# Last FFN in a written order, two weight tiles ahead, with three column groups computed from seven products in both halves of their sum

## The chip, the cores and the metric

The kernel runs on one core of one Trainium2 chip. The metric is the time of one execution on the device in microseconds, the median of several runs.

## The reference, and what of it matters here

The program is one residual block of a streaming encoder on 256 rows (tokens) of width 2048, all in float32: an FFN, a token mixer and a second FFN, each followed by a layer norm, with shift, scale and gate rows made from a conditioning vector. The change lies in the second FFN, the last stage:

```python
y = _swiglu(modulate(x, 2), ffn2_w13[l], ffn2_w2[l])          # (silu(g) * v) @ w2
x = _layer_norm(ALPHA * x + FFN_WEIGHT * gate[:, 2, None, :] * y, ln_g[l, 2], ln_b[l, 2])
```

`_swiglu` multiplies the 256x2048 activations u by w13 (2048 x 11264: 5632 gate columns g, 5632 value columns v), takes silu(g) times v, and multiplies the result by w2 (5632 x 2048).

## The kernel before, in words

**Tiles and products.** Weights come from memory as tiles of 128 partitions x 2048 float32, 1 MB each: four slices of 128 rows by 512 columns. A float32 product is made of three fast ones. `split` (L100-112) writes a tile's high part with a cast on ScalarE (L108, names h...) and its low part with a subtraction on VectorE (L110, names l...). `mov_t` (L285-295) multiplies one weight tile with the activations of one token half (128 tokens): four slices times three matmuls (high by high, high by low, low by high), so 12 matmuls of 512 columns. I call those 12 a block product. `mov_w` does it for both token halves: 24 matmuls. There are three buffers each for high and low parts and four for raw tiles (`raw_tile`), two buffers of tag "row", six large ones of tag "slot", eight PSUM banks.

**The last FFN** is `ffn(2, ...)` (L654). Its 5632 hidden columns are 11 column groups b = 0 to 10 of 512. For each group g and v are made, silu(g) times v goes through TensorE transposes (`turn_one`, L806) into a stationary layout (a high part by ScalarE at L816, a low part by VectorE at L817), and, two at a time, turned groups meet w2 (`x_tile`, L734: one w2 tile, 24 matmuls; after every second one the two PSUM banks are added to `yacc`). Groups 0, 1 and 10 are made plainly (`rows_block`, 16 block products). Groups 2 to 9 go through `fast_block` (L704). There the first 1024 of the 2048 input rows ("quad 0": two row tiles of g and two of v, against two token halves) are computed with seven block products in place of eight, in the manner of Strassen and Winograd: sums of weight tiles are formed on VectorE (L756, L761, L766, L775, four a group) and sums of activations once, in `sums` (L683). The other 1024 rows ("quad 1") are plain: eight block products. So a group has 15 block products, four `x_tile`, eleven plus four splits.

**The order.** The instructions of `fast_block` go to the engines through plain handles (`nc.vector`, `nc.scalar`), so that the planner, which places instructions by its own costs, may set them in another order on VectorE, ScalarE and SyncE than the program writes them; TensorE's products are pinned with the handle `T`. The handles `V`, `A`, `G`, `T`, `Q` (class `Pinned`, L120) keep program order. Beside the products `tick` (L213) feeds in 16 tiles of the conditioning matrix ("ada", a multiply-and-reduce on VectorE, L210) at the rate `FFN2_RATE`. `closing` (L1026) multiplies the last three groups with w2, and `boundary` ends with the layer norm.

Of the kernel before, what the change touches and what calls it, by code (L numbers as in the profile page):

```python
# [16 lines left out]
P = 128  # L17
D = 2048
# [23 lines left out]
FFN2_RATE = 0.5  # L42
# [3 lines left out]
FAST = range(2, 10)  # L46


class Held:
# [4 lines left out]
    def __getitem__(self, key):  # L54
        return self.tile[key]
# [3 lines left out]
def block_kernel(ctx: ExitStack, tc: tile.TileContext, a: dict, out: bass.AP):  # L59
# [19 lines left out]
    wide = [False]  # L79
    n_raw = [1]  # L80
# [13 lines left out]
    def load(src, name, into=None, raw=None):  # L94

        tick()
        raw = raw or raw_tile("r" + name)
        queue().dma_start(raw, src)
        return raw, name, into
# [40 lines left out]
    def queue():  # L140

        return Q if wide[0] else nc.sync
# [511 lines left out]
    def ffn(s, w13, w2, start, following=None):  # L654
# [8 lines left out]
        b0 = RAMP // 4 if start else 0  # L663
# [5 lines left out]
        def rows_block(b, passed=None):  # L669

            i = 8 * (b - b0)
            if passed:
                pg, pv = passed[0], met(passed, w13[4:8], f"fv{s}")
            else:
                pg = [bank(f"fg{s}{b}{t}") for t in range(NT)]
                for k in range(4):
                    end = mov_w(pg, load_w(w13[i + k], f"fg{s}_{b}{k}"), uh, ul, k * 4, k == 0, k == 3)
                    if k in (1, 2):
                        turn_one(end)
                pv = [bank(f"fv{s}{b}{t}") for t in range(NT)]  # L680
                for k in range(4):
                    mov_w(pv, load_w(w13[i + 4 + k], f"fv{s}_{b}{k}"), uh, ul, k * 4, k == 0, k == 3)
# [5 lines left out]
        def sums():  # L688

            nc.gpsimd.dma_start(xd, x.tile)  # L690
            f = raw_tile("sums").rearrange("p (a b) -> p a b", b=P)
            for t in range(NT):
                tk = slice(t * P, (t + 1) * P)
                nc.vector.tensor_add(f[:, 8 * t:8 * t + 8, :], uh[:, 0:8, tk].bitcast(F32), ul[:, 0:8, tk].bitcast(F32))
            a11, a12, a21, a22 = (f[:, 4 * i:4 * i + 4, :] for i in range(4))
            nc.vector.tensor_add(a22, a21, a22)
            nc.vector.tensor_sub(a21, a11, a21)
            nc.vector.tensor_sub(a11, a22, a11)
            nc.vector.tensor_sub(a12, a12, a11)
            both = big.tile([P, 2, KT, P], F32R, tag="x", name="ws")  # L700
            nc.scalar.copy(both[:, 0], f)
            nc.vector.tensor_sub(both[:, 1], f, both[:, 0].bitcast(F32))
            return both[:, 0], both[:, 1]

        def restore():
            x.tile = tokens("x1")
            for t in range(NT):
                nc.gpsimd.dma_start(x[:, t, :], xd[:, t, :])
            scale_x()

        def fast_block(b, wh, wl):

            i = 8 * b
            gi = 4 * b // GRP - 1
            s2_, s4_, s3_, s1_ = 0, 4, 8, 12
            p1, p5 = bank(f"fa{b}"), bank(f"fb{b}")
            py = {}

            def part(ps, hl, h, k0, t, first, last):
                return mov_t(ps, hl, *h, k0, t, first, last, T, skip_group_check=not first and ps in (p1, p5))  # L720

            def fresh(k, row=False):
                return load(w13[i + k], f"fw{s}_{b}{k}", None, row_tile(f"fw{b}{k}") if row else None)

            def halves(tile, w=""):
                return split((tile[0], tile[1] + w, None), nc.scalar, nc.vector)

            def kept(ps, tag, w):
                to = sm.tile([P, 512], F32, tag=tag, bufs=2, name=f"{w}{s}{b}")
                nc.scalar.copy(to, ps)  # L730
                return to

            def x_tile(m):
                n, k = b % 2 * 2 + m // 2, m % 2  # L734
                if not k:
                    py[n] = [bank(f"py{gi}_{n}_{t}") for t in range(NT)]
                kg = 2 * gi + k
                end = mov_w(py[n], load_w(w2[kg * 4 + n], f"w2{s}_{kg}_{n}"), *hts[gi], k * 4, not k, k == 1, T)
                if k:
                    c = slice(n * 512, (n + 1) * 512)  # L740
                    for t in range(NT):
                        if gi == 0:
                            evac.append(nc.scalar.copy(yacc[t][:, c], py[n][t]))
                        else:
                            nc.vector.tensor_add(yacc[t][:, c], yacc[t][:, c], py[n][t])
                return end

            u, w = (uh, ul), (wh, wl)
            ta = fresh(0, True)
            end = part(p1, halves(ta), u, 0, 0, True, True)  # L750
            turn_one(end)
            f1 = kept(p1, "u", "fs")
            tc_ = fresh(4, b >= 4)
            end = x_tile(0)
            turn_one(end)
            nc.vector.tensor_sub(ta[0], tc_[0], ta[0])  # L756
            part(p5, halves(ta, "p"), w, s1_, 0, True, True)
            f5 = kept(p5, "gy", "ft")
            td = fresh(5)
            x_tile(1)  # L760
            nc.vector.tensor_sub(ta[0], td[0], ta[0])  # L761
            part(p1, halves(ta, "q"), w, s2_, 0, False, True)
            f2 = kept(p1, "gy", "fv")
            part(p5, halves(td), w, s4_, 0, False, False)
            x_tile(2)
            nc.vector.tensor_sub(tc_[0], td[0], tc_[0])  # L766
            part(p1, halves(tc_, "q"), w, s3_, 0, False, True)
            f3 = kept(p1, "u", "fu")
            p2, p4 = bank(f"fc{b}"), bank(f"fd{b}")
            tb = fresh(1)  # L770
            part(p2, halves(tb), u, 4, 0, True, False)
            g2_ = load_w(w13[i + 2], f"fw{s}_{b}2")
            part(p2, g2_, u, 8, 0, False, False)
            part(p4, g2_, u, 8, 1, True, False)
            nc.vector.tensor_sub(tb[0], tb[0], ta[0])  # L775
            part(p4, halves(tb, "p"), u, 4, 1, False, False)
            g3_ = load_w(w13[i + 3], f"fw{s}_{b}3")
            part(p2, g3_, u, 12, 0, False, True)
            part(p4, g3_, u, 12, 1, False, True)
            nc.vector.tensor_add(f1, f1, p2)  # L780
            nc.scalar.activation(f1, f1, AF.Silu)
            nc.vector.tensor_add(f3, f3, p4)
            nc.scalar.activation(f3, f3, AF.Silu)
            x_tile(3)
# [4 lines left out]
            if 4 * b // GRP not in hts:  # L789
                new_h(4 * b // GRP)  # L790
# [768 lines left out]
```

## Time and profile before

| what | us |
|---|---|
| median of 3 runs | 1881.79 (1880.12 to 1884.59) |
| the profiled execution | 1882.46 |
| its span, first to last instruction | 1880.7 |
| start of group 2 in it (first `fa` matmul) | 1242.96 |
| start of group 10 in it (first `fg` matmul of the group) | 1759.44 |

The profile shows one execution. Times in its rows count from the first instruction. A row of a timeline has the start, the duration, the engine, the line and the tiles, and in brackets how long the engine had been idle and what it had waited for. Busy times of TensorE overlap, so the distance from one matmul's start to the next is its price, not its duration. The chain of work that ended last names at each moment what the end depended on.

### The profile page before, as it was taken

The numbers are of one execution on the slowest core, as the hardware profiler recorded it, in microseconds if no ns is written. First come the engines' busy times: TensorE is split into PE (matmuls) and PEld (weight loads), VectorE is DVE, ScalarE is ACT, GpSimd is POOL, SyncE is SP. The second block draws the span as 40 slices with busy tenths as digits, with TensorE's granted clock in tenths as the row PEclk, the third lists the DMA queues.
The fourth block names the chain that finished last, engine by engine and source line by source line (L and its number), as shares of the span: only waits on it lengthen the run. The fifth ranks groups of instructions, "written<-read, shape, count | busy, mean of one in ns | idle before, by whom it ended". The sixth has DMA issues, their size and how long they took to land.

```text
span 1880.7 us, 21240 instructions
## 1 busy us (share of the span) xinstructions
PE 1861.4 (99%) x8495; PEld 1526.0 (81%) x8495; DVE 1561.3 (83%) x1467; ACT 895.1 (48%) x847; POOL 43.2 (2%) x68
## 2 busy tenths in 40 slices
PE   8999999999999999999999999999999999999998
PEld 5788888888888888788888887878778888888886
DVE  6899998887887987889997877789887788778776
ACT  4543444533334335756644356454544455545441
POOL 0000000000000000100000121000000000000000
PEclk9999999999999999999999999999999999999999
DMA  9989889999899987478687574768855654564662
GB/s 377 417 354 366 319 311 347 357 348 355 344 357 355 339 331 269 148 276 296 244 317 296 203 264 182 268 246 300 307 210 190 224 212 168 202 224 186 239 224 90
DMA packets 74931, 520.06 MB, mean 277 GB/s; under 512 B 8736, under 2 KB 8912, under 8 KB 13520
## 3 DMA queue, kind: packets, MB, share of 16 engines
q1 hardware_dynamic: 72144, 507.54, 71.6%
q0 software_dynamic: 960, 7.37, 1.0%
q10 hardware_dynamic: 1728, 3.80, 0.6%
q8 instruction: 66, 1.08, 0.2%
q14 instruction: 33, 0.27, 0.0%
HBM read 514.46 MB, written 4.22 MB: 276 GB/s over the span
## 4 chain that ended last, share of the span: by engine, by line
PE 92%; DVE 4%; DMA 2%; issue 1%; ACT 1%; POOL 0%; POOLq 0%; DVEq 0%; SPq 0%; ACTq 0%
PE py L133 9%; PE pj L281 5%; PE fa L133 5%; PE fb L133 4%; PE fc L133 3%; PE fd L133 3%; PE py L293 3%; PE py L294 3%; PE py L292 3%; PE pj L283 3%; PE fg L293 3%; PE fg L294 3%; PE fg L292 3%; PE fv L293 3%; PE fv L292 3%; PE fv L294 3%
## 5 line engine op out<-in xcount | busy, mean ns | idle before, releaser
L210 DVE CUSTOM_DVE_ANT_0 ada<-ada,scb,badac 128x2048 f32<-128x2048 f32 x110 | 258.0, 2345 | 39.5 <-DMA ada<-in_w_ada 39.0
L108 ACT CAST hw<-rw 128x2048 fp32r<-128x2048 f32 x81 | 155.1, 1914 | 218.0 <-DMA rw<-in_w 60.6
L110 DVE TENSOR_TENSOR lw<-rw,hw 128x2048 fp32r<-128x2048 f32 x81 | 185.1, 2287 | 55.8 <-ACT hw L108 55.0
L110 DVE TENSOR_TENSOR lfw<-rfw,hfw 128x2048 fp32r<-128x2048 f32 x48 | 109.9, 2289 | 17.2 <-ACT hfw L108 17.2
L281 PE MATMUL pj<-u,hs 128*128 128x512 f32 x512 | 122.5, 391 | 0.0
L108 ACT CAST hra<-rra 128x2048 fp32r<-128x2048 f32 x38 | 72.6, 1914 | 102.2 <-DMA rra<-in_w_r 43.1
L108 ACT CAST hfw<-rfw 128x2048 fp32r<-128x2048 f32 x48 | 91.9, 1915 | 47.8 <-PE py L133 28.2
L281 PEld LDWEIGHTS pj<-u,hs 128*128 128x128 f32 x512 | 94.3, 188 | 18.4
L133 PE MATMUL py<-lw,hth 128*128 128x512 f32 x256 | 99.8, 390 | 2.1 <-DVE lw L110 2.1
L133 PE MATMUL py<-hw,hth 128*128 128x512 f32 x256 | 100.4, 392 | 0.0
L293 PE MATMUL py<-lw,hth 128*128 128x512 f32 x256 | 99.8, 390 | 0.1
L294 PE MATMUL py<-hw,htl 128*128 128x512 f32 x256 | 99.7, 390 | 0.0
L133 PE MATMUL py<-hw,htl 128*128 128x512 f32 x256 | 99.7, 389 | 0.0
L292 PE MATMUL py<-hw,hth 128*128 128x512 f32 x256 | 97.3, 392 | 0.0
L108 ACT CAST hfg<-rfg 128x2048 fp32r<-128x2048 f32 x28 | 53.6, 1914 | 86.1 <-DMA rfg<-in_w 48.8
L108 ACT CAST hs<-rs 128x2048 fp32r<-128x2048 f32 x32 | 61.0, 1908 | 68.7 <-PE pj L281 53.6
L293 PE MATMUL fg<-lfg,u 128*128 128x512 f32 x224 | 87.4, 390 | 0.1
L294 PE MATMUL fg<-hfg,u 128*128 128x512 f32 x224 | 87.3, 390 | 0.0
L293 PE MATMUL fv<-lfv,u 128*128 128x512 f32 x224 | 87.2, 389 | 0.0
L294 PE MATMUL fv<-hfv,u 128*128 128x512 f32 x224 | 87.1, 389 | 0.0
L108 ACT CAST hfv<-rfv 128x2048 fp32r<-128x2048 f32 x28 | 53.6, 1913 | 66.7 <-DMA rfv<-in_w 41.3
L292 PE MATMUL fg<-hfg,u 128*128 128x512 f32 x224 | 84.5, 392 | 0.0
(727 smaller groups left out, 4764.4 us busy)
## 6 DMA issues: line engine op xcount, KB each, us to landing
ada<-in_w_ada SPq DMA_DIRECT2D x138, 1024.0 KB, 6.5
rw<-in_w SPq DMA_DIRECT2D x81, 1024.0 KB, 5.5
rfw<-in_w SPq DMA_DIRECT2D x50, 1024.0 KB, 4.8
rra<-in_w_r SPq DMA_DIRECT2D x45, 1024.0 KB, 7.4
rs<-in_w_s SPq DMA_DIRECT2D x32, 1024.0 KB, 5.0
rfg<-in_w SPq DMA_DIRECT2D x28, 1024.0 KB, 6.7
rfv<-in_w SPq DMA_DIRECT2D x28, 1024.0 KB, 5.5
rwo<-in_w_out SPq DMA_DIRECT2D x16, 1024.0 KB, 4.8
```

The source lines that it names most:

```text
L108: act.copy(cut(hi, w), like(raw[:, w], hi))
L110: low.tensor_sub(cut(lo, w), like(raw[:, w], lo), cut(hi, w).bitcast(F32))
L133: self.last = getattr(self.engine, op)(*args, **kw)
L210: vec.tensor_tensor_reduce(raw[:, c], raw[:, c], scb[:, c], 1.0, base, ALU.mult, ALU.add, to)
L281: nc.tensor.matmul(ps, hi[:, k * P:(k + 1) * P], both(k), start=k == 0, stop=False)
L283: nc.tensor.matmul(ps[:, 0:S], lo[:, k * P:(k + 1) * P], uh[:, k, :], start=False, stop=k == KT - 1)
L292: pe.matmul(o, acth[:, k0 + j, tk], cut(hi, w), start=first and j == 0, stop=False, **kw)
L293: pe.matmul(o, acth[:, k0 + j, tk], cut(lo, w), start=False, stop=False, **kw)
L294: end = pe.matmul(o, actl[:, k0 + j, tk], cut(hi, w), start=False, stop=last and j == 3, **kw)
```

## The change

`ffn` keeps only the first FFN. The last FFN becomes `last_ffn`, which writes out every step and gives every instruction but those of the gate rows to the pinned handles. A step is a triple: what TensorE does, what prepares its weight tile (load, sums, split), and what follows it. `flow` emits the steps; before a step goes to TensorE, the tiles of that step and of the next two that have one are prepared (`AHEAD = 3`). `beside` hangs other work (the ada tiles, the sums of activations, the gated sum) behind the preparation of certain tiles.

Groups 2, 3, 5, 7 and 9, and now 10 as well, have seven products in quad 0 (`S4`, `S2`). Groups 4, 6 and 8 (`DOUBLE`, plan `D6`) have seven in both quads, 14 block products, and take six of the pair's eight w2 tiles (X); the plan `S2` after them takes the other two. Quad 1 needs its own sums of activations (`sums(1, in_slot)`), kept in one slot and one row buffer. In the groups of `BY_DMA` two of the four sums of weight tiles a quad are made by a GpSimd DMA that adds a tile in memory onto one in SBUF (c + d for P7, a + b for P4); in the others VectorE makes all four. x goes to memory scaled and comes back by an adding DMA onto the gated `yacc`.

```diff
-FAST = range(2, 10)
+DOUBLE = (4, 6, 8)
+BY_DMA = DOUBLE
+AHEAD = 3
+S4 = "P1 t X t P5 X P6 P3 X P7 P2 G P4 G X V V"
+S2 = "P1 t G t P5 X P6 P3 G P7 P2 X P4 V V"
+D6 = "P1 t X t P5 X P6 P3 X P7 P1 P2 X P5 P4 X P6 P3 P2 X P7 P4"
...
+        def step(pe, prep=None, after=None):
+            steps.append((pe, prep, after))
+            n_prep[0] += prep is not None
+        def beside(fs, at=0, every=1):
+            for k, f in enumerate(fs):
+                extras.setdefault(n_prep[0] + at + k * every, []).append(f)
...
+        def flow():
+            hls, late, n, m = {}, [], 0, 0
+            for i, (pe, prep, after) in enumerate(steps):
+                for f in late:
+                    f()
+                while n < len(steps) and (n <= i or len(hls) < AHEAD):
+                    if steps[n][1]:
+                        hls[n] = steps[n][1]()
+                        for f in extras.get(m, ()):
+                            f()
+                        m += 1
+                    n += 1
+                pe(hls.pop(i, None))
+                late = after() or [] if after else []
...
+        def halves(tile, w="", into=None):
+            return split((tile[0], tile[1] + w, into), A, V)
...
+        def turn():
+            def pe(_):
+                b, t, sg = to_turn.pop(0)
...
+                    T.transpose(now[0][2][:, j * P:(j + 1) * P], sg[:, j * P:(j + 1) * P], ident)
+            def after():
+                b, t, ps = now.pop()
...
+                A.copy(hth[:, :, tk], ps)
+                V.tensor_sub(htl[:, :, tk], ps, hth[:, :, tk].bitcast(F32))
...
+            for n in ns:
+                yield lambda n=n: x_step(kgs[0], n, pss, 0, False)
+                yield lambda n=n: x_step(kgs[1], n, pss, 1, True, lambda: evac(n))
...
+            def keep(key, tag, q, bk="1"):
+                if q == 0:
+                    f[key] = sm.tile([P, 512], F32, tag=tag, bufs=2, name=f"f{key}{s}{b}")
+                    A.copy(f[key], ps[bk])
+                else:
+                    V.tensor_add(f[key], f[key], ps[bk])
...
+                elif w == "P7":
+                    keep("3", "u", q)
+                    if q:
+                        V.tensor_add(f["5"], f["5"], f["3"])
+                elif w == "P5" and q == quads - 1:
+                    keep("5", "gy", 0, "5")
+                elif w == "P3" and q:
+                    V.tensor_add(f["2"], f["2"], f["5"])
+                    V.tensor_add(f["2"], f["2"], ps["3"])
+                elif w == "V" and q:
+                    V.tensor_add(f["2"], f["2"], ps["5"])
+                    V.tensor_add(f["5"], f["5"], ps["1"])
...
+                        V.tensor_add(f[g], f[g], ps[key])
+                        A.activation(f[g], f[g], AF.Silu)
...
+                        def product(t=t, g=g, v=v):
+                            V.tensor_mul(f[g], f[g], f[v])
+                            to_turn.append((b, t, f[g]))
...
+            def prep(w, q):
+                if w == "P1":
+                    W["a", q] = raw(q, 0, q == 0)
+                    return halves(W["a", q])
+                if w == "P5":
+                    W["c", q] = raw(q, 4, row_c)
+                    a, c = W["a", q], W["c", q]
+                    V.tensor_sub(a[0], c[0], a[0])
+                    hl = halves(a, "p")
+                    if dma:
+                        G.dma_start(c[0], w13[i + 2 * q + 5], accum_op=ALU.add)
+                    return hl
+                if w == "P6":
+                    W["d", q] = raw(q, 5, q == 1)
+                    a, d = W["a", q], W["d", q]
+                    V.scalar_tensor_tensor(a[0], a[0], -1.0, d[0], op0=ALU.mult, op1=ALU.subtract)
+                    hl = halves(a, "q")
+                    if dma:
+                        G.dma_start(a[0], w13[i + 2 * q + 1], accum_op=ALU.add)
+                    return hl
+                if w == "P3":
+                    return halves(W["d", q])
+                if w == "P7":
+                    c, d = W["c", q], W["d", q]
+                    if not dma:
+                        V.tensor_add(c[0], c[0], d[0])
+                    return halves(c, "q")
+                if w == "P2":
+                    W["b", q] = raw(q, 1)
+                    return halves(W["b", q])
+                if w == "P4":
+                    a = W["a", q]
+                    if not dma:
+                        V.tensor_add(a[0], a[0], W["b", q][0])
+                    return halves(a, "r")
...
+        def gated_sum(t):
+            def go():
+                for n in range(4):
+                    c = slice(n * 512, (n + 1) * 512)
+                    V.tensor_mul(yacc[t][:, c], yacc[t][:, c], gate[:, c])
+                G.dma_start(yacc[t], xd[:, t, :], accum_op=ALU.add)
...
+        beside([scaled(0), scaled(1), ada, ada, ada, *sums(0, in_x), ada, ada])
+        first_group(nxt.pop())
+        plain_group(1)
+        beside([ada] * 9, 3, 3)
+        for b in range(2, n_b - 1, 2):
+            kgs = (b - 2, b - 1)
+            if b in DOUBLE:
+                xs = x_steps(kgs, range(4))
+                fast_group(b, 2, xs, D6, False)
+                fast_group(b + 1, 1, xs, S2, False)
+            else:
+                xs = x_steps(kgs, range(4))
+                for i in range(2):
+                    fast_group(b + i, 1, xs, S4, b > 2 and not DOUBLE)
+            if b == 2 and DOUBLE:
+                beside(sums(1, in_slot), -4)
+        beside([lambda: gate_rows(s, 0.5)], -4)
+        beside([gated_sum(0), gated_sum(1)], 4, 2)
...
+        es = end_steps()
+        fast_group(n_b - 1, 1, es, S2, False)
```

In a plan P1 to P7 are the seven products of a quad, in the order of their use, G and V the plain row tiles of quad 1 (both token halves, 24 matmuls), X a w2 tile, t the transposes of one token half of the group before. P5 and P6 always need a sum on VectorE ahead of their split; P7 and P4 need one where the DMA doesn't make it.

More of the change, by code (lines that the diff above doesn't have):

```diff
@@ L140, in queue @@
     def queue():
-        return Q if wide[0] else nc.sync
+        return Q if wide[0] or fixed[0] else nc.sync
     @contextmanager
@@ L662, in ffn @@
         evac = []
-        b0 = RAMP // 4 if start else 0
+        b0 = RAMP // 4
         sts = new_stats(s)
@@ L705, in restore @@
[L705 to L784, printed above, removed]
-            vs = [load_w(w13[i + 4 + k], f"fw{s}_{b}{4 + k}") for k in (2, 3)]
-            for t, ps in enumerate((p5, p1)):
-                for k in range(2):
-                    part(ps, vs[k], u, 8 + 4 * k, t, False, k == 1)
-            if 4 * b // GRP not in hts:
-                new_h(4 * b // GRP)
-            for t, h, v, ps in ((0, f1, f2, p5), (1, f3, f5, p1)):
-                nc.vector.tensor_add(v, v, ps)
-                nc.vector.tensor_mul(h, h, v)
-                to_turn.append((b, t, h))
@@ L973, in g1 @@
             grp = groups[gi]
-            if start and gi == 2:
+            if gi == 2:
                 new_h(gi)
@@ L982, in g1 @@
                 return
-            if start and gi == 3:
+            if gi == 3:
                 for t in range(NT):
```

330 lines of the change are left out of this document (243 added, 87 removed).

## The prediction

> **What bounds the kernel now.** I read the page's head first, then the busy times by stage, the chain that ended last inside the last FFN, and the timelines of VectorE and ScalarE there.
>
> ```profile
> span 1880.7 us, 21240 instructions
> PE 1861.4 (99%) x8495; PEld 1526.0 (81%) x8495; DVE 1561.3 (83%) x1467; ACT 895.1 (48%) x847; POOL 43.2 (2%) x68
> ```
>
> The stages, cut at the starts of groups 2, 5, 6 and 10 (columns: PE, weight load, DVE, ACT, POOL busy, clock, DMA share, GB/s):
>
> ```profile
> 1242.90:1441.80 198.90, 194.00 (x854) 158.49 (x853) 170.62 (x108) 102.47 (x77) 0.00 (x0) 0.99 0.68 254
> 1441.80:1505.30 63.50, 63.50 (x286) 52.60 (x285) 50.49 (x32) 32.76 (x23) 0.00 (x0) 1.00 0.54 199
> 1441.80:1759.20 317.40, 317.40 (x1422) 262.82 (x1421) 250.56 (x158) 167.34 (x118) 2.21 (x4) 1.00 0.56 206
> ```
>
> From group 5 to the end of group 9 TensorE never stops (317.40 of 317.40), and VectorE, the next one, is busy 79% (250.56). In groups 2 to 4 TensorE loses some time. The chain gives the prices of the steps:
>
> ```profile
> 1242.96 2.72 PE fa L133 x12
> ...
> 1436.38 8.16 PE fa L133 x36
> 1444.54 0.44 PE th L814 x4
> 1444.98 5.47 PE py L133 x24
> 1450.45 0.44 PE th L814 x4
> 1450.88 2.75 PE fb L133 x12
> 1453.63 5.44 PE py L133 x24
> ...
> 1508.47 5.47 PE py L133 x24
> ```
>
> A block product of 12 matmuls is 2.72 us, a step of 24 is 5.44, four transposes 0.44. A group is 15 x 2.72 + 4 x 5.44 + 0.88 = 63.4; the two `py` rows stand 63.49 apart. The `fa` row of 36 holds 24 matmuls of group 4, so group 5 begins at 1441.82, and groups 2 to 4 took 198.86 where 3 x 63.49 = 190.5 would do: 8.4 are lost there.
>
> **Removed.** Three groups and group 10 lose a block product each: 4 x 2.72 = 10.9 us of TensorE, all on the path, since TensorE is the path. If the new order also ends the loss in groups 2 to 4, 8.4 more go. So 19.3 is the most that can be won.
>
> **What the order costs.** VectorE and ScalarE now take their instructions as written. In the planner's order a sum of weight tiles stands far ahead of its split:
>
> ```profile
> 1446.74 2.29 DVE L110 TENSOR_TENSOR lw<-rw,hw 128x2048 fp32r<-128x2048 f32 x1
> 1448.94 2.29 DVE L761 TENSOR_TENSOR fw<-rfw,fw 128x2048 f32<-128x2048 f32 x1
> 1451.14 1.28 DVE L817 TENSOR_TENSOR htl<-th,hth 128x512 fp32r<-128x512 f32 x2
> 1453.35 2.29 DVE L110 TENSOR_TENSOR lfw_50q<-fw,hfw_50q 128x2048 fp32r<-128x2048 f32 x1 [0.93 <-ACT hfw_50q L108]
> 1456.39 0.69 DVE L745 TENSOR_TENSOR yacc<-yacc,py 128x512 f32<-128x512 f32 x1 [0.75 <-PE py L133]
> 1456.99 2.29 DVE L110 TENSOR_TENSOR lfw<-rfw,hfw 128x2048 fp32r<-128x2048 f32 x1
> ```
>
> ```profile
> 1450.92 0.59 ACT L816 CAST hth<-th 128x512 fp32r<-128x512 f32 x1 [3.42 <-PE th L814]
> 1451.40 1.92 ACT L108 CAST hfw_50q<-fw 128x2048 fp32r<-128x2048 f32 x1
> ```
>
> Back to back, a 128x2048 step of VectorE is 2.20 (1446.74 to 1448.94), a 128x512 step 0.60 (1456.39 to 1456.99); a cast is 1.92 and its low part starts 0.03 later. Behind the sum at 1448.94 the planner put two `htl`. In the new text sum, cast and low part are written one after the other, so VectorE stands idle for the cast, about 1.97 us, at every sum that it makes.
>
> By count alone, a pair (D6 + S2): TensorE has 14 x 2.72 + 6 x 5.44 + 0.88 = 71.6 and 7 x 2.72 + 6 x 5.44 + 0.88 = 52.6, together 124.2, where the pair before has 127.0. VectorE has 33 low parts and 8 sums (41 x 2.20 = 90.2), 28 small steps (16.8) and 8 idle casts (15.8): 122.8, or 99%. It can keep up only if it never waits for anything else.
>
> It does wait, and I followed its queue step by step. At the start of D6 (time 0: the last V of the group before ends on TensorE) the queue reads: two adds and two products (4 x 0.60 = 2.4), P5's sum 2.20, cast 1.97, low part 2.20, X2's low part 2.20, the first `htl` 0.60, P6's sum 2.20, cast 1.97, low part 2.20, the second `htl` 0.60: 18.5, and some 0.2 to see the end of V and to hand on: 18.7. The second `htl` stands behind the whole preparation of P6, because `flow` prepares P6 before it emits the second t. On TensorE P1, t, X1, t, P5 and half of X2 take 2.72 + 0.44 + 5.44 + 0.44 + 2.72 + 2.72 = 14.5, and the second half of X2 reads that `htl`. TensorE waits 4.2 us, in every even group; before, both `htl` came at 1451.14, ahead of the `py` step at 1453.63 that needs them. Queued behind it on VectorE stand P3's low part, X2's adds and all that follows.
>
> Further on in the pair, the same way: P6' of D6 needs its d in the row buffer, which P4 gives back when its low part is done (49.2 after the start). Its load, sum, cast and low part then follow with nothing between:
>
> ```profile
> L781 ACT ACTIVATE fs<-fs 128x512 f32<-128x512 f32 x8 | 5.0, 630 | 17.7 <-DVE fs L780 17.7
> ```
>
> ```profile
> rfw<-in_w SPq DMA_DIRECT2D x50, 1024.0 KB, 4.8
> xd<-x POOLq DMA_DIRECT2D x1, 2048.0 KB, 11.1
> x<-xd POOLq DMA_DIRECT2D x2, 1024.0 KB, 7.4
> ```
>
> 49.2 + 4.8 + 2.2 + 1.97 + 2.3 = 60.5, while TensorE is ready at 57.9: 2.6. In S2 the last V steps: P4's sum starts behind X8's low part (117.1), 2.2 + 1.97 + 2.2 to 123.5, then the add and the silu that close the first sum (1.2), and only then the cast and low part for V (4.2): 128.9, TensorE ready at 126.2: 2.7. The others, each from where VectorE then stands: P5' of D6, low part of X4 done at 39.9, an add, then sum, cast and low part (0.6 + 6.4): 46.9, TensorE ready at 46.0: 0.9. P5 of S2: the adds that close D6 hold VectorE until 85.3, and 6.4 more make 91.7 against 89.2: 2.5. P6: X's low part, `htl`, then again 6.4: 100.9 against 99.8: 1.1. P7: two low parts and 6.4 behind 101.8: 112.6 against 112.0: 0.6. With three small ones D6 comes to 79.7 and S2 to 60.1: 139.8, or 15.6 of waits a pair, 46.8 for three.
>
> Hidden is the traffic: D6 loads 14 tiles and adds 4 by transfers, 18 x 1.05 MB in 79.7 us, 237 GB/s, less than groups 2 to 4 had (254, at a DMA share of 0.68). SyncE's loads stay two or more preparations ahead of their casts but for that one d; if they didn't, each would cost up to the 4.8 of a load. ScalarE has 33 casts a pair and is under two thirds busy. P6's sum is a scalar-tensor-tensor now, which the trace has in no such size: I price it like the subtraction, at most like the ada step below (0.15 more).
>
> Groups 2 and 3 (S4) keep 15 products and gain nine ada tiles at fixed places and the second set of activation sums:
>
> ```profile
> L210 DVE CUSTOM_DVE_ANT_0 ada<-ada,scb,badac 128x2048 f32<-128x2048 f32 x11 | 25.8, 2348 | 8.8 <-DMA ada<-in_w_ada 8.8
> ```
>
> VectorE there has 2 x (19 x 2.20 + 8 x 0.60 + 4 x 1.97) = 109, the ada 9 x 2.3 = 20.7 and 8.8 for the sums: 138, against 127 on TensorE, so 11 at least. By the queue the waits are 10.7 in group 2 (5.3 at X2, with an ada tile in that chain too) and 10.5 in group 3 (P6 3.5, P7 2.9, P4 2.3, V 1.8): 21.2. Group 10 in S2 has the 7.6 of that plan and about half of the gated sums' eight multiplies (4.8): 10. Groups 0 and 1 take 5.44 on TensorE a step and at most 2.20 + 2.35 on VectorE: nothing.
>
> **The clock.** Before, TensorE waited once for 2.58 us, and what came behind ran slowly:
>
> ```profile
> 1240.00:1280.00 40.00, 37.42 (x163) 30.42 (x162) 35.42 (x23) 20.46 (x17) 0.00 (x0) 0.96 0.61 219
> ```
>
> ```profile
> 1263.02 0.50 PE L133 MATMUL fa<-lfw_20q,ws 128*128 128x512 f32 x1 [2.58 <-DVE lfw_20q L110]
> ...
> 1264.17 1.05 PE L133 MATMUL fa<-hfw_20q,ws 128*128 128x512 f32 x2
> 1265.02 0.63 PE L133 MATMUL fa<-lfw_20q,ws 128*128 128x512 f32 x1
> ```
>
> Matmuls 0.43 apart instead of 0.227 in a stretch whose granted clock is 0.96: 0.04 x 40 = 1.6 us for that wait. Four X2 waits of 4 us or more could cost 6.4; behind a VectorE that is late anyway I take half, 3. The Trainium skill ("TensorE: Matmul & The Clock Gate", section "Part 1: The HAM clock gate") has the clock halve after an idle window of about 3.4 us; the row shows it after 2.58. By the page's window as a least idle time the X2 waits, which two matmuls divide, would cost nothing, and the sum would be 3 lower.
>
> **The sum.** The profiled execution took 1882.46 (span 1880.7 and 1.8 around it). -10.9 - 8.4 + 21.2 + 46.8 + 10 + 3 = +61.7: 1944; it stands 0.7 above the median of the runs, so 1943.5 on that scale, and I say 1944.
>
> **The rivals.**
> *Faster.* The queue's waits are filled after all: only the counts bind. Then -19.3 + 11 = -8, 1874. For it: 122.8 is below 124.2, and ScalarE is half idle. Against: the chain at the start of D6 alone costs 3 x 4.2. It decides if all waits in groups 4 to 10 stay under 8 us together.
> *Only the openings wait.* The counts, and the X2 chain in groups 4, 6 and 8: -8 + 12.6 = +5, and 3 for the clock: 1890. For it: the waits further on hang on estimates of where VectorE stands; against: they follow from the same queue.
> *The transfers are late.* The row tile a' is summed by GpSimd's DMA from P6's low part (60.6) on, and P4's cast wants it at 72.5: 11.9 us. No adding transfer is in the trace. It moves 1 MB and reads its target besides; the nearest rows are 7.4 for 1 MB and 11.1 for 2 MB, so I take 9 to 11, and nothing is late. At 20 us, each of three D6 waits 8 more: +25, 1969. The Trainium skill ("DMA: Bandwidth & Descriptors", "Anatomy of one DMA") gives 2.0 us and bytes / 436e3 for such a transfer, as an estimate 4.4 for 1 MB, which would strike this rival; the row for 1 MB is 7.4.
>
> **How the numbers follow.** The forecast has 0.72, the late transfers 0.10, the openings alone 0.10, the faster case 0.08. The range goes from halfway between the count case and the forecast, 1909, to the late transfers with a clock cost at more waits, 1974. A measurement of this kernel tells about 0.2% (3.8 us) from no change. Faster has its 0.08; within 0.2% lies a little of the openings case (a few us less than 1890), 0.04; the rest is slower, 0.88.
>
> **What would show it.** Right: TensorE busy well under 100% from group 2 to 9; a pair near 140 us between the first P1 products of groups 4 and 6; VectorE idle about 1.9 us before each low part that follows a sum, released by ScalarE; in X2 of groups 4, 6 and 8 a wait of some 4 us that ends on `htl`; a d load that waits for the row buffer. Wrong: pairs of 124 to 127 us; `htl` done before X2's second half; VectorE under 85% busy with TensorE full; or ScalarE waiting for GpSimd's transfers at P7 or P4, which would put the loss on them.

## The result, and the profile after

| kernel | median us | runs | range |
|---|---|---|---|
| before | 1881.82 | 4 | 1880.12 to 1884.59 |
| after | 1972.41 | 4 | 1971.89 to 1973.68 |

The change makes the kernel slower: ratio 1.0481, 95% interval 1.0463 to 1.0499, 90.6 us more. The profiled execution of after took 1972.67, its span is 1970.9. Group 2 starts at 1244.01 in it (1.05 later than before), group 10 at 1827.46 (68.0 later), and the end comes 90.2 later. So groups 2 to 9 cost 67.0 us more, and what follows from group 10 on 22.2 more.

The head of after's page:

```profile
span 1970.9 us, 21259 instructions
PE 1894.8 (96%) x8447; PEld 1533.9 (78%) x8447; DVE 1606.7 (82%) x1498; ACT 916.4 (46%) x864; POOL 54.2 (3%) x80
```

TensorE has 48 matmuls fewer, the four block products that the change removes, and yet is busy 33 us longer, above all since matmuls run slowly behind waits. The share of the chain that ended last, by engine, tells who sets the pace now (TensorE held 92% of it before):

```profile
PE 70%; DVE 15%; issue 6%; ACT 6%; DMA 2%; POOL 0%; DVEq 0%; ACTq 0%; POOLq 0%; SPq 0%
```

The busy times by stage, cut at the starts of groups 2, 4, 6, 8 and 10 (columns: length, PE, weight load, DVE, ACT, POOL, clock, DMA share, GB/s):

```profile
1242.90:1393.86 150.96, 138.64 (x574) 110.52 (x573) 120.10 (x78) 69.88 (x55) 0.00 (x0) 0.94 0.57 219
1393.86:1539.58 145.72, 134.06 (x557) 106.12 (x556) 110.99 (x71) 70.28 (x49) 3.49 (x4) 0.95 0.62 206
1539.58:1683.10 143.52, 132.82 (x557) 105.67 (x556) 109.31 (x69) 70.29 (x49) 3.42 (x4) 0.96 0.62 205
1683.10:1827.46 144.36, 132.86 (x559) 105.61 (x557) 109.38 (x69) 70.34 (x50) 4.57 (x6) 0.96 0.63 211
1827.46:1970.90 143.44, 120.19 (x493) 93.93 (x491) 102.52 (x101) 45.37 (x36) 5.12 (x6) 0.94 0.46 154
```

A pair (two groups) took 127.0 before and takes 145.7, 143.5 and 144.4. In none of these stages is any engine full: TensorE stands still for some 11 us a pair, VectorE for 35, and ScalarE for half the time. That looks like a stage bound by the order in which the engines wait for each other; the experiments test it.

VectorE at the start of D6 (group 4), where the prediction followed its queue step by step (columns: start, duration, engine, line, operation, tiles; in brackets the idle time and what ended it):

```profile
1397.36 2.28 DVE L142 TENSOR_TENSOR fw<-rfw,fw 128x2048 f32<-128x2048 f32 x1
1401.70 2.29 DVE L142 TENSOR_TENSOR lfw_40p<-fw,hfw_40p 128x2048 fp32r<-128x2048 f32 x1 [2.06 <-ACT hfw_40p L142]
1403.99 2.29 DVE L142 TENSOR_TENSOR lw<-rw,hw 128x2048 fp32r<-128x2048 f32 x1
1406.19 0.68 DVE L142 TENSOR_TENSOR ht<-th,ht 128x512 fp32r<-128x512 f32 x1
1406.80 2.28 DVE L142 SCALAR_TENSOR_TENSOR fw<-fw,rfw 128x2048 f32<-128x2048 f32 x1
1411.12 2.29 DVE L142 TENSOR_TENSOR lfw_40q<-fw,hfw_40q 128x2048 fp32r<-128x2048 f32 x1 [2.04 <-ACT hfw_40q L142]
1413.33 0.68 DVE L142 TENSOR_TENSOR ht<-th,ht 128x512 fp32r<-128x512 f32 x1
```

P5's sum, 2.06 idle for its cast, two low parts, the first `ht`; then P6's sum, 2.04 idle, its low part, and only at 1413.33 the second `ht`. On TensorE the second X waits for it:

```profile
1411.63 0.50 PE L142 MATMUL py<-hw,ht 128*128 128x512 f32 x1 [2.05 <-ACT ht L142]
1411.96 0.44 PE L142 MATMUL py<-lw,ht 128*128 128x512 f32 x1
1414.07 1.22 PE L142 MATMUL py<-hw,ht 128*128 128x512 f32 x2 [1.67 <-DVE ht L142]
1415.09 0.63 PE L142 MATMUL py<-lw,ht 128*128 128x512 f32 x1
1415.51 1.05 PE L142 MATMUL py<-hw,ht 128*128 128x512 f32 x2
...
1418.50 0.63 PE L142 MATMUL f<-hfw_40q,ws 128*128 128x512 f32 x1
1418.93 0.44 PE L142 MATMUL f<-lfw_40q,ws 128*128 128x512 f32 x1
1419.21 0.63 PE L142 MATMUL f<-hfw_40q,ws 128*128 128x512 f32 x2
```

2.05 + 1.67 = 3.72 us of waiting, and behind it matmuls 0.43 apart instead of 0.227 until 1418.9. From 1262 us on the recorded clock has 16 such slow stretches ahead of the kernel's last 3 us, 13 of 3.41 us and three of 6.83, 65 us together.

The adding transfers of after (median from issue to landing in the last column):

```profile
rfw<-in_w POOLq DMA_DIRECT2D x9, 1024.0 KB, 8.1
fw<-in_w POOLq DMA_DIRECT2D x3, 1024.0 KB, 8.8
yacc<-xd POOLq DMA_DIRECT2D x2, 1024.0 KB, 10.1
```

### The profile page after: what moved, and what is told of

The parts are those of the page before. It is cut to its first block, busy times and chain, and to the rows that moved or that the text cites. A ratio compares the mean times of both kernels' runs of the same rounds, so it can differ in the third digit from the quotient of the medians.

```text
span 1970.9 us, 21259 instructions
## 1 busy us (share of the span) xinstructions
PE 1894.8 (96%) x8447; PEld 1533.9 (78%) x8447; DVE 1606.7 (82%) x1498; ACT 916.4 (46%) x864; POOL 54.2 (3%) x80
## 4 chain that ended last, share of the span: by engine, by line
PE 70%; DVE 15%; issue 6%; ACT 6%; DMA 2%; POOL 0%; DVEq 0%; ACTq 0%; POOLq 0%; SPq 0%
PE f L142 9%; PE pj L290 5%; PE py L142 4%; PE py L302 3%; PE py L301 3%; PE py L303 3%; PE pj L292 3%; DVE fw L142 2%; PE fg L302 2%; PE fg L303 2%; PE fg L301 2%; PE fv L301 2%; PE fv L302 2%; PE fv L303 2%; PE rv L765 2%
## 5 line engine op out<-in xcount | busy, mean ns | idle before, releaser
L142 PE MATMUL py<-hw,ht 128*128 128x512 f32 x656 | 217.9, 404 | 18.4 <-ACT ht L142 10.2
L142 PEld LDWEIGHTS py<-hw,ht 128*128 128x128 f32 x656 | 127.2, 195 | 49.6 <-ACT ht L142 12.1
L142 PE MATMUL py<-lw,ht 128*128 128x512 f32 x328 | 131.9, 402 | 0.9 <-DVE lw L142 0.9
L142 DVE CUSTOM_DVE_ANT_0 ada<-ada,scb,badac 128x2048 f32<-128x2048 f32 (+1 forms) x50 | 110.8, 2216 | 4.3 <-DMA ada<-in_w_ada 4.1
L302 PE MATMUL py<-lw,hth 128*128 128x512 f32 x256 | 99.8, 390 | 0.1
L303 PE MATMUL py<-hw,htl 128*128 128x512 f32 x256 | 99.7, 390 | 0.0
L301 PE MATMUL py<-hw,hth 128*128 128x512 f32 x256 | 97.3, 392 | 0.0
L119 DVE TENSOR_TENSOR ls<-rs,hs 128x2048 fp32r<-128x2048 f32 x32 | 73.0, 2282 | 11.7 <-ACT hs L117 11.6
L142 DVE TENSOR_TENSOR lra<-rra,hra 128x2048 fp32r<-128x2048 f32 x29 | 66.3, 2286 | 9.7 <-ACT hra L142 7.6
L292 PE MATMUL pj<-u,ls 128*128 128x256 f32 x512 | 66.4, 283 | 0.0
L117 ACT CAST hfg<-rfg 128x2048 fp32r<-128x2048 f32 x20 | 38.3, 1915 | 60.1 <-DMA rfg<-in_w 55.5
```

Source lines behind the costliest of these rows:

```text
L117: act.copy(cut(hi, w), like(raw[:, w], hi))
L119: low.tensor_sub(cut(lo, w), like(raw[:, w], lo), cut(hi, w).bitcast(F32))
L142: self.last = getattr(self.engine, op)(*args, **kw)
L292: nc.tensor.matmul(ps[:, 0:S], lo[:, k * P:(k + 1) * P], uh[:, k, :], start=False, stop=k == KT - 1)
L301: pe.matmul(o, acth[:, k0 + j, tk], cut(hi, w), start=first and j == 0, stop=False, **kw)
L302: pe.matmul(o, acth[:, k0 + j, tk], cut(lo, w), start=False, stop=False, **kw)
```

## The experiments

The theory was that the written order costs the time: VectorE and ScalarE take what is written, stand idle for each other behind every sum, and the transposed values stand behind the preparation of P6. The rivals: the second quad itself (more sums and splits), late adding transfers, or the clock. Each run has its own median of before beside it, 1881.8 to 1884.7; ratios are to that.

| run | median us | ratio, 95% interval |
|---|---|---|
| no group doubled | 1945.28 | 1.0335 (1.0320 to 1.0351) |
| sums on VectorE | 2004.67 | 1.0648 (1.0632 to 1.0664) |
| transposes first | 1957.32 | 1.0395 (1.0380 to 1.0411) |
| sums ahead | 1943.44 | 1.0324 (1.0307 to 1.0342) |
| waits filled | 1968.42 | 1.0465 (1.0449 to 1.0480) |
| reordered | 1929.03 | 1.0256 (1.0239 to 1.0273) |
| reordered, none doubled | 1900.81 | 1.0101 (1.0086 to 1.0117) |
| reordered, sums on VectorE | 1959.17 | 1.0410 (1.0394 to 1.0426) |
| reordered, none doubled, gated tile early | 1895.26 | 1.0064 (1.0047 to 1.0081) |
| reordered, without quad 1's sums | 1925.07 | 1.0219 (1.0204 to 1.0234) |
| end stage alone | 1959.61 | 1.0402 (1.0387 to 1.0418) |
| reordered, transposes later | 1953.86 | 1.0371 (1.0348 to 1.0393) |

### No group doubled

```diff
-DOUBLE = (4, 6, 8)
+DOUBLE = ()
```

> The written order without the second quad: DOUBLE and BY_DMA empty, all of groups 2 to 9 in S4 (15 block products). Theory of the queue (VectorE stands idle for the cast behind each sum, and the second htl stands behind P6's preparation): three block products come back, 8.2 us of TensorE, but a pair of S4 groups has 114 us of VectorE queue against 127 of TensorE, so odd groups wait about 2 us and even ones 5 to 6 with the X2 chain and a slow clock behind it: a pair takes 135 to 137 against the 144.5 measured, 24 less for three pairs, and the sums of the second quad go (3): about 1945, still 60 slower than before. Rival of the doubling (the second quad and its sums are the cost): pairs are back at 127, 1915 to 1920. Rival of the transfers (the adding transfers come late): the same 1915 to 1920.

1945.28, as the theory said. 63 us of the loss stay without a single second quad and without adding transfers of weight tiles: they belong to the written order, with what it fixes (the places of the ada tiles, the new end). The second quad adds the other 27. Both are parts of the loss.

### All sums on VectorE

```diff
-BY_DMA = DOUBLE
+BY_DMA = ()
```

> BY_DMA empty: VectorE makes the sums for P7 and P4 in groups 4, 6 and 8 too, four more a group, no adding transfer for weights. Theory of the queue: each is 2.20 us and an idle cast of 1.97 in a queue that already sets the pace, 16.7 a pair less what VectorE idles while it waits for TensorE: 8 to 14 more a pair, about 2005 in all (1995 to 2015). Rival of the transfers: they were late, so the time falls or stays: 1972 or less.

2004.67: without the transfers it is 32 us slower. They take work off VectorE. Nor are they late: from group 2 to the end of group 9 no wait of ScalarE in after's trace ends on one.

### Both transposes ahead of the first X

```diff
-S4 = "P1 t X t P5 X ..."
+S4 = "P1 t t X P5 X ..."
-D6 = "P1 t X t P5 X ..."
+D6 = "P1 t t X P5 X ..."
```

> In S4 and D6 both transposes t stand ahead of the first X (P1 t t X P5 ...), so the second htl is emitted ahead of P6's preparation; nothing else changes. Theory of the queue: the wait inside X2 in groups 2, 4, 6 and 8 (3.3 to 4.1 us in the profile) and the slow clock behind it (about 1.7) go, and later waits stay: 4 x 5 less, about 1952 (1947 to 1958). Rival of the count (VectorE's queue is full over the pair, so a wait that is taken away comes back at the next low part): under 5 us less, 1967 or more.

1957.32, 15 us less: 4.3 in groups 2 and 3, 12.8 in the three pairs (141.1, 140.2, 139.6), that is 3.4 to 4.8 each; from group 10 on 1.6 were given back. It is at the upper end of what was expected. The X2 chain costs about what the trace shows for it (waits of 3.3 to 3.7 us a pair and slow matmuls behind them), and it is a sixth of the loss.

### Each sum emitted one preparation earlier

The sum for P5, P6, P7 and P4 (with its load) goes out behind the preparation of the step before, so that VectorE has a low part between the sum and its cast.

```diff
+                        follow = next((x for x in steps[n + 1:] if x[1]), None)
+                        if follow and follow[3]:
+                            follow[3]()
```

> Each sum on VectorE (P5, P6, and P7, P4 where no transfer makes them) is emitted, with its load, right behind the preparation of the step before, ahead of that step's evacuations, and only the split at its old place: the same instructions, another order. The cast then needs no sum in front of it. Theory of the queue: the eight idle casts a pair (15.8 us) go, and the chain at the start of D6 falls from 18.7 to about 12.4 us, under the 14.5 that TensorE takes: pairs fall from 144.5 to 127 to 131, groups 2 and 3 from 150 to 130 to 135, group 10 by 6 to 8: 1895 to 1920. Rival of the doubling or of the transfers: the order of sum and split matters little, 1955 or more. Rival of the count: VectorE's busy time alone is 107 a pair, so it predicts the same as the queue here.

1943.44: missed, 29 us less instead of 50 or more. The waits at X2 of groups 4, 6 and 8 are gone, and so is P6's in group 3. But the second P6 of D6 still waits 2.2 us and the V of groups 5, 7 and 9 still 2.1, and other waits came, first of all at the transposes, which wait for the product that closes a group, now behind the sums on VectorE (TensorE's waits there from 1242 on: us in all, times, longest):

```profile
PE th L142 <- DVE f L142: 6.7, 5, 2.3
```

### The waits filled with matmuls

Small matmuls on a spare bank (24 between the halves of the second X of each pair's first group, 14 ahead of P5 and of the first V of groups 5, 7 and 9) keep TensorE busy where it waits.

```diff
+                    idle(bank(f"id{kg}"), 24)
...
+                idle(bank(f"id{w}{b}"), 14)
```

> The changed kernel with TensorE kept busy where the profile shows it waiting long: 24 small 128x128 matmuls (0.12 us each in the opening rows of the kernel before, 2.8 us together) between the two halves of X2 in groups 2, 4, 6 and 8, and 14 (1.6 us) ahead of P5 and ahead of the first V in groups 5, 7 and 9; their result is used by nothing. Theory that the halved clock is on the path: the ten or so half-clock stretches behind these waits (3.4 us, or 6.8, at half speed: 1.7 or 3.4 us lost each) go, 12 to 20 us less: 1952 to 1961. Rival, that VectorE's queue sets the time and hides a slow TensorE: 0 to 4 less, 1968 or more; if the small matmuls outlast the waits, it gets slower than 1973.

1968.42: the mean clock rises from 0.982 to 0.992, of the 65 us at half clock 31 are left, and the time falls by 4. The forecast of 12 to 20 missed. But the run doesn't settle what the half clock costs, because the fills lasted longer than meant: each small matmul leaves two records, and a fill took 5.3 us in place of 2.8, or 3.05 in place of 1.6. The X2 of group 4, VectorE's low part for it (done at 1411.69) and the fill, which TensorE is still busy with until 1412.38:

```profile
1411.01 0.68 DVE L142 TENSOR_TENSOR ht<-th,ht 128x512 fp32r<-128x512 f32 x1
```

```profile
1407.10 5.52 PE L142 MATMUL id<-ident 128*128 128x128 f32 x48
1412.38 0.48 PE L142 MATMUL py<-hw,ht 128*128 128x512 f32 x1
```

At the ten fills TensorE goes on 0.35 to 1.1 us after its tile was ready, 5.7 us together. So 17 us of lost speed came back, the fills themselves took up at least some 6 of them, and 4 were won. How many of the others a late VectorE would have cost anyway is open: the half clock costs 4 us or more, and shorter fills weren't tried.

### Reordered, with and without the second quad, and with all sums on VectorE

The sums ahead as above; what closes a group behind the next preparation; X last in S4 and S2; in the last stage the products that need group 10 last.

```diff
+S4 = "P1 t X t P5 X P6 P3 X P7 P2 G P4 G V V X"
+S2 = "P1 t G t P5 X P6 P3 G P7 P2 V P4 V X"
+D6 = "P1 t X t P5 X P6 P3 X P7 P1 P4 P2 X P5 X P6 P3 P2 X P7 P4"
...
+            for n, k in ((0, 0), (0, 1), (1, 0), (1, 1), (2, 0), (2, 1), (0, 2), (1, 2), (2, 2)):
```

> e4_sums_ahead with the remaining waits of its trace taken away by order alone: the add and silu that close a gate half, and the products, are emitted behind the next preparation and not ahead of it; the last X of S4 and S2 stands at the end, so that TensorE has work while the products are made; P4 of quad 0 stands right behind P1 of quad 1 in D6, so that the row buffer for d comes free sooner; the w2 tile that needs group 10's transposes comes later in the end. Theory of the queue: pairs fall from 137 to 126 to 131, groups 2 and 3 from 142.6 to 134 to 140, the end from 143 to 130 to 138: 1885 to 1912. Rival of the count: VectorE is busy 109 of a pair with or without this, and two tiles of lookahead are too few for D6: pairs stay above 133, 1925 or more.

> e6_reordered without the second quad (DOUBLE and BY_DMA empty, all in S4). Theory of the queue: a pair of S4 groups then takes 127 to 130, of which 127 is TensorE's own work: within 10 us of e6_reordered, which saves 8.2 of TensorE and pays for it with a fuller VectorE. Rival of the doubling: 20 or more faster than e6_reordered.

> e6_reordered with all sums on VectorE (BY_DMA empty; in D6 P2 of quad 0 stands ahead of P1 of quad 1, since the sum for P4 then needs b). Theory of the queue: four more sums a D6 are 8.8 us of VectorE a pair, without idle casts now; VectorE's sum for a pair goes from 107 to 116 of 124: 2 to 8 more a pair than e6_reordered, 6 to 24 in all. Rival of the transfers (they delay P7 and P4): not slower than e6_reordered.

1929.03, 1900.81 and 1959.17 (the last with P2 ahead of the second P1 in D6). The first missed what the theory wanted: pairs of 134 to 138 us. The second shows why. Without doubling the same order runs TensorE full. The stage of groups 4 and 5 in the reordered kernel without doubling, and that of groups 6 and 7 in the one with it:

```profile
1383.72:1511.42 127.70, 127.56 (x569) 104.79 (x568) 98.70 (x61) 65.95 (x47) 0.00 (x0) 1.00 0.51 198
```

```profile
1523.33:1658.74 135.41, 127.29 (x557) 102.06 (x556) 108.90 (x70) 70.20 (x49) 3.43 (x4) 1.00 0.65 218
```

So doubling costs 28 us in this order, 27 in the change's; it saves three products (8.2 us), so some 36 us of waits and slow matmuls come with it, 12 a pair. And the transfers are again worth 30 us.

### The gated tile earlier; the end stage alone

From group 10 on, the last product needs a w2 tile that is multiplied by the gate, and it was prepared after everything else. In the reordered kernel without doubling it now follows the first of the last three X; in the changed kernel it is prepared behind the last X tile, and the products that need group 10 come last.

```diff
-            for n, k in (..., (0, 2), (1, 2), (2, 0), (2, 1), (2, 2)):
+            for n, k in (..., (2, 0), (2, 1), (0, 2), (1, 2), (2, 2)):
...
+        beside([lambda: gated(0)], -1)
         flow()
         fine[0] = True
-        gated(0)
```

> The reordered kernel without doubling (1900.8), with the gated w2 tile that the last product needs first taken out of its place behind everything and prepared after the first of the last three X steps. There TensorE waited 6.0 us for it (5.63 for the cast, 0.40 for the low part). Theory of the queue: the end stage is long because of where work stands on VectorE, so these 6.0 us go, less up to 2 that come up as other waits: 1894 to 1898. Rival: the gated tile is late because all of VectorE's work at the end is, and the moved work delays the adds into x by as much: 1899 or more.

> The changed kernel (1972.4) with two edits in its last stage alone: the gated w2 tile that the last product needs first is prepared behind the last X step's own tile instead of after everything, and the X steps that need group 10's transposed values come after those of the other two groups. Group 10 to the end took 143.4 us against 121.3 before; of it 4.9 stand at X(0,2) behind the second transposes and 4.5 at the gated tile. Theory: both are the order of the queues, 5 to 10 less, 1962 to 1967. Rival: VectorE is late there by its amount of work, 0 to 3 less, 1969 to 1972.

1895.26 and 1959.61: 5.5 and 12.8 us less. Both are the order of the queues. The second gain is larger than expected: from group 10 on the waits below are gone, and with them most of the half clock there (13.7 us of it ahead of the last 3 us, 3.4 after the edit). In the changed kernel TensorE had waited at these places from group 10 on (us in all, times, longest), and after the edit none of these rows is left:

```profile
PE tl L301 <- ACT hw22l L142: 3.6, 1, 3.6
PE py L142 <- ACT ht L142: 2.8, 1, 2.8
...
PE py L142 <- DVE ht L142: 1.2, 1, 1.2
PE tl L302 <- DVE lw22l L142: 0.9, 1, 0.9
PE py L142 <- DVE lw L142: 0.9, 1, 0.9
```

### Without quad 1's sums

```diff
-                    V.tensor_sub(a[0], c[0], a[0])
+                    if not q:
+                        V.tensor_sub(a[0], c[0], a[0])
```

and the same for P6's sum, in the reordered kernel. The kernel leaves these two sums out, so it computes other values.

> The reordered kernel with doubling (1929.0), with the two sums that VectorE makes for quad 1 (c - a and -a - d) left out, so the values that it multiplies there are not the reference's; all loads, splits, transfers and products stay. A pair is 136.4 us with doubling and 127.8 without. Theory: doubling costs because it fills VectorE's queue; two sums of 2.2 and the casts that two of them wait for (up to 4) go from each pair: three pairs x 4.4 to 8.4 = 13 to 25 less, 1904 to 1916. Rival: doubling costs by something else that it brings (the adding transfers, the held row buffers, the longer chains of PSUM sums): at most 3 us a pair less on TensorE's path, 1920 or more.

1925.07: 4 us less where 13 to 25 were expected. The theory that doubling costs mainly by the amount of VectorE's work falls. The stage of groups 6 and 7 in this run:

```profile
1523.35:1656.00 132.65, 127.22 (x557) 103.45 (x556) 104.31 (x68) 70.39 (x49) 3.42 (x4) 0.99 0.66 222
```

VectorE has 4.6 us less to do than in the reordered kernel, and the pair is 2.8 shorter; the last one is 1.7 shorter, and the first isn't shorter at all (138.1 against 138.2).

### The transposes later

In the same reordered kernel the longest waits of a pair stand at the transposes: 3.0 in S2 behind D6, where both sums close at its very end, 1.7 to 2.1 in D6.

```diff
+S2 = "P1 t G P5 t X P6 P3 G P7 P2 V P4 V X"
+D6 = "P1 X t t P5 X P6 P3 X P7 P1 P4 P2 X P5 X P6 P3 P2 X P7 P4"
```

> The reordered kernel with doubling (1929.0), with only the places of the transposes changed: in S2 the second stands behind P5 instead of ahead of it, in D6 both stand behind the first X and P5 ahead of the second X. Leaving out quad 1's sums took only 2.7 us from a pair of 135.4, so most of the 8.6 that a pair has above one without doubling lies elsewhere: in its trace TensorE waits 2.7 and 1.7 at the transposes that follow a closed double sum (release by VectorE's product) and 0.8 at the X behind them, and one half-clock stretch follows. Theory: the doubling's price is this late closing of both sums at the end of D6, so later transposes save 4 to 7 a pair: 1907 to 1918. Rival: the closing is late because VectorE as a whole is, and the wait comes up again at the next step that it feeds: 1923 or more.

1953.86, 25 us more, and neither reading was tested cleanly: the waits at the transposes of the pairs are gone, but a new one is longer. ScalarE in group 6 of this run:

```profile
1535.63 1.91 ACT L142 CAST hfw_60p<-fw 128x2048 fp32r<-128x2048 f32 x1 [4.63 <-DVE fw L142]
1540.50 0.59 ACT L142 COPY f<-f 128x512 f32<-128x512 f32 x1 [2.96 <-PE th L142]
1540.98 1.91 ACT L142 CAST hw<-rw 128x2048 fp32r<-128x2048 f32 x1
1547.51 1.90 ACT L142 CAST hfw_60q<-fw 128x2048 fp32r<-128x2048 f32 x1 [4.61 <-DVE fw L142]
1549.31 1.07 ACT L142 CAST ht<-th 128x512 fp32r<-128x512 f32 x2
```

The copy of P1's sum waits for a buffer that the transposes give back (2.96), VectorE's next sum comes late by that, and the casts of both transposed halves stand behind the cast that waits for this sum (4.61). TensorE's X waits 6.29 for them, in each pair. The wait did come up again at the next step, as the rival had it, but on ScalarE's queue.

## Why the prediction was right, and where it was short

**Sign and mechanism: right.** 1972.4 lies in the range, near its upper end. The queue at the start of D6 came as written: idle 2.06 and 2.04 us for the casts (forecast 1.97), the second `ht` behind P6's low part, X2's wait 3.72 (forecast 4.2), worth 3.4 to 4.8 us a pair, slow matmuls included, when the order is changed. Most of the other waits named are there too, and mostly a little shorter: P6' of D6 waits 2.10 (forecast 2.6), its sum first 1.5 for a d load that had to wait for the row buffer; P5' 0.85 (0.9), P5 of S2 2.06 (2.5), V 2.10 (2.7). Those of S2's P6 and P7 (forecast 1.1 and 0.6) are missing, but for 0.8 at P6 in group 9. P6's scalar-tensor-tensor took 2.28, like the subtraction. P6' of D6 on VectorE, with the wait for d, the sum, the idle cast and the low part:

```profile
1451.57 2.29 DVE L142 SCALAR_TENSOR_TENSOR rfw<-rfw,fw 128x2048 f32<-128x2048 f32 x1 [1.51 <-DMA fw<-in_w]
1455.88 2.29 DVE L142 TENSOR_TENSOR lfw_42q<-rfw,hfw_42q 128x2048 fp32r<-128x2048 f32 x1 [2.03 <-ACT hfw_42q L142]
```

**The pairs: too low by 4.7 each.** Forecast 139.8, measured 144.5 on average: 14 us in three pairs. Of the 4.7, 2.7 are in D6 (82.4 on average, forecast 79.7) and 2.0 in S2 (62.1, forecast 60.1). It isn't the named waits: between the starts of groups 4 and 6 TensorE stands idle for 11.7 in all, where 15.6 stood. That pair exceeds the count of 124.2 by 21.5; 6.8 of the rest are 13.65 us at half clock, and 3.0 weren't followed. So the forecast put the waits too high and the slow matmuls far too low, and the two errors partly cancel. What a pair would take at full clock no run shows cleanly: with the waits filled, most of the half clock in the pairs went and they took 2.3 us less together, but the fills outlasted the waits.

**The clock: priced too low.** The sum had 3 us, from the X2 waits of four groups. The trace has 16 slow stretches, 65 us, which is 32 us of lost speed. From group 2 on TensorE stands idle for 69.4 us, where before has 11.8, and loses 31 us more to the half clock than before. How much of that loss adds to the time is open; filling the waits won 4, and that is a least value.

**Groups 2 and 3: the time right, partly by luck.** 75.6 and 74.2 measured, 74.2 and 74.0 forecast from 63.5 plus 10.7 and 10.5. But TensorE stands idle only 6.4 and 5.9 there; most of the rest is half clock, 10.2 and 6.8 us long, so 5.1 and 3.4 of lost speed, which the forecast had not put there.

**The end: 15 us short.** From the start of group 10 on it took 143.4, where 121.3 before, less 2.7 for the product, plus 10, makes 128.6. The term for group 10 priced its own steps and the gated sums' multiplies, and never followed the queue past it. The transposes of group 10 with an X that needs them straight behind, and the gated tile at the very end, cost 9.4 in the rows above; the edit of the end stage won back 12.8. These 15, the 14 of the pairs, 1.6 in groups 2 and 3 and 1.05 ahead of them, less the 3 that the sum had for the clock, are, but for rounding, the 28.5 between the forecast's +61.7 and the +90.2 measured in the span.

**The rivals.** *Faster by counts* fell: the counts bind nowhere. *Openings only* fell: they are worth 15 of 90. *Late transfers* fell: 8.1 to 8.8 us (medians) for an adding transfer, where 9 to 11 was my estimate and 11.9 the time there was, and taking them away costs 30 to 32. The time of that rival, 1969, was hit by accident. The Trainium skill ("DMA: Bandwidth & Descriptors", "Anatomy of one DMA") gives 4.4 as an estimate, and the trace shows about twice that.

**What makes up the 90 us.** By the runs, 63 are the written order with what it fixes, and 27 the second quad. Of the 63, 50 are undone by another order of the same steps (1945.3 to 1895.3). The 12 that are left against before are in groups 2 and 3 (140.8 where 127.0 would do) and from group 10 on (125.9 against 121.3), with 2.2 in groups 4 to 9, less the 8.4 that before itself loses in groups 2 to 4: 13.8 + 4.6 + 2.2 - 8.4 = 12.2. That the nine ada tiles in groups 2 and 3 are the cause of the 13.8 is argued, from the 9 x 2.3 us on VectorE that the prediction gave them; spreading them over the later groups wasn't tried.

**What stays open.** Why the second quad brings 12 us of waits and slow matmuls a pair. Leaving out two of its sums takes away 0.1 to 2.8 of a pair, so the amount of VectorE's work is the smaller part. In the reordered kernel's trace the waits sit where both sums close together at the end of D6 (3.0 at the transposes behind it) and at those in D6 (1.7 to 2.1), but moving these transposes only moved the wait. ScalarE stands 46 us in the same stages before silus that wait for VectorE's closing add, with the next casts behind them, against 30 us without doubling:

```profile
ACT f L142 <- DVE f L142: 45.9, 14, 5.2
```

```profile
ACT f L142 <- DVE f L142: 30.3, 10, 3.3
```

(the waits of ScalarE from 1242.9 to 1830, first the reordered kernel, then the same without doubling: us in all, times, longest). This fits a loop of two in-order queues that wait for each other, but no run took the silus out of that queue. No run gave the new steps to the plain handles either, so what the planner would have made of them is not known. No kernel tried was faster than before.

## What to carry to other kernels

Work removed from the bounding engine was worth nothing here, where the engines that feed it waited for each other. Before writing an order by hand, follow each queue through a whole period, and put something between a sum and the cast of it that the same engine can do meanwhile. An order by hand has to be followed to its last instruction: here the unexamined end stage cost 15 us, and two moved steps gave 13 of them back. When a wait is removed by moving its step, ask which queue the step now stands in; two of these runs mostly moved the wait.

## What the runs showed of the hardware

The clock was halved after waits of about 2 us, not only after the 2.58 us of before: 2.05, two matmuls and 1.67 in group 4 with 0.43 a matmul behind them. The Trainium skill ("TensorE: Matmul & The Clock Gate", "Part 1: The HAM clock gate") speaks of at least one idle window of about 3.4 us; no wait in these rows is that long, so as a least time for a single wait this trace doesn't bear it out. The slow stretches themselves, 3.41 and 6.83 us long, fit one and two windows of its length.

What counted was where a wait fell. In the recorded clock of every run the slow stretches from group 2 on start whole multiples of 3.41 us apart (to 0.002 us). With the time cut into these windows, half clock follows in after's trace behind every window at full clock in which TensorE stood idle for more than 1.82 us, and behind none with less; over all 14 traces the border lies between 1.71 and 1.86. So the same wait can cost the clock or not. The second P6 of group 4 (first two rows) waits 1.83, of which 0.15 lie ahead of the edge of a window and 1.68 behind it, and its matmuls go on 0.23 apart; the V of group 5 (the others) waits 1.83 inside one window, and half clock follows at 1528.2:

```profile
1458.23 0.50 PE L142 MATMUL f<-lfw_42q,ws 128*128 128x512 f32 x1 [1.83 <-DVE lfw_42q L142]
1459.27 0.39 PE L142 MATMUL f<-hfw_42q,ws1l 128*128 128x512 f32 x1
```

```profile
1527.14 0.50 PE L142 MATMUL f<-lfw_5V,u 128*128 128x512 f32 x1 [1.83 <-DVE lfw_5V L142]
1528.99 0.63 PE L142 MATMUL f<-lfw_5V,u 128*128 128x512 f32 x1
1529.42 1.05 PE L142 MATMUL f<-hfw_5V,u 128*128 128x512 f32 x2
```

An adding transfer of 1 MB from memory took 8.1 to 8.8 us onto a weight tile and 10.1 onto `yacc`, against 7.4 for a plain one on the same queue before (medians from issue to landing, beside other traffic).
